# Turning the new keys and values into rows: matmuls with the identity, or square blocks on VectorE with stores that put them in place

## The chip, the cores and the metric

The kernel runs on one core of a Trainium2 chip. The metric is the time of one execution on the device, in microseconds, given as the median of three runs. The profile and the trace come from one further execution, taken by the hardware profiler. The engines are named as in the profile: PE is TensorE, DVE is VectorE, ACT is ScalarE, POOL is GpSimd, and SP is SyncE, which issues most of the DMAs.

## The reference

The reference computes one layer of a streaming encoder for 512 prompt frames and 64 sample frames of width 2048, all in 32-bit floats. Cut to what matters here, it is:

```python
proj = rmsnorm(x, g_norm1) @ w_in
q, k, v, gb, gc, hc = split(proj)              # q, k, v: 8 heads x 128; the rest: 8 groups x 128
q, k = rmsnorm(q, g_q), rmsnorm(k, g_k)        # per head
o_attn = stick_breaking(q, [k_past, k], [v_past, v])
o_conv = gb * conv3_causal(gc * hc)
x = x + concat(rmsnorm(o_attn), rmsnorm(o_conv)) @ w_out
x = x + (silu(h2 @ w_gate) * (h2 @ w_up)) @ w_down     # h2 = rmsnorm(x, g_norm2)
return x, k, v, new_conv
```

The new keys and values `k` and `v` are outputs of their own, as `k_prompt`, `v_prompt` (512 frames) and `k_sample`, `v_sample` (64 frames), each with one row of 128 numbers for a frame and a head. The change is about how these rows are made.

## The kernel before, in words

All activations are kept transposed: features lie on the 128 partitions, and the 576 frames (512 of the prompt, 64 of the sample) along the free axis. A product is a chain of matmuls with a tile of weights as the stationary operand and 288 frames as the moving one. For accuracy each operand is split into a high and a low part, so that each product of a weight tile with frames takes three matmuls; the high part is cast by ACT (L227) and the low one is a subtraction on DVE (L228). The large products use a Strassen-like scheme with seven partial products for each block of weights, and `prepare` (L357) makes the split weights of a product four products ahead of its use.

The work goes in stages. First the input is turned and the values of heads 0 to 3 are computed. Then, up to about 575 us, follow the 22 units listed in `HEADS_A` (L53): pairs of column blocks of `w_in`, for query and key of a head ("qk"), two value heads ("v"), or the convolution ("gh", "gb"). Then the output projection is computed with the attention woven into it, head by head, and at last the feed-forward network.

A finished key or value head is a tile `E` of 128 features by 576 frames. Its rows for the outputs are made by `tokens` (L804), a generator that is started with a lag when a head is done. It turns four blocks of 128 frames with matmuls against the identity into a bank of PSUM (L808), has ACT copy them to an SBUF tile `tok` (L810), and stores that with one DMA (L812). Three ticks later it turns the last 128 frames (L817), which ACT copies to `tokz` (L819), and stores the 64 sample rows (L820). For values it also stores both into `v_dram` (L814, L822), a buffer in device memory, from which the attention reads them again (`fetch_v`, L1031, called for head 0 at L1038 and for each later head at the end of the one before). `v_dram` holds, for each head, 128 partitions of five blocks of 128. `tokens` runs for the eight key heads and for value heads 4 to 7. Value heads 0 to 3 go through `plain_tokens` (L785), which scales the rows by the norm while ACT copies them; it too writes `v_dram`.

The tiles `tok` and `tokz` come from a pool with the tag "hl" and three buffers, which also serves squares, norms and the convolution (`hl_tile`, L628). A buffer is free again when its last reader, for a stored tile the DMA, is done.

PE's instructions run in the order in which the program writes them. The order of the others (ACT, DVE, POOL, SP) is set by the planner of the framework in the stages concerned here, from priorities and from its own view of what is ready. Each engine then works in its order and waits on semaphores. A small `Pipeline` (L73) counts ticks, one for every three matmuls of a product, and starts side work at given ticks.

At the seam to the attention stage the program calls `load_qk(0)` (L1035), `split_qk` (L1036), `load_cached_keys(0)` and `fetch_v(0)`. Their DMAs are issued by SP, as are the stores of `tokens` and the loads of `w_out` (L183). The first scores of a head are the matmuls at L1161.

Of the kernel before, what the change touches and what calls it, by code (L numbers as in the profile page):

```python
# [10 lines left out]
F32 = mybir.dt.float32  # L11
# [5 lines left out]
P = 128  # L17
TP = 512
TS = 64
T = TP + TS  # L20
HALF = T // 2
HALVES = ((0, HALF), (HALF, T))
D = 2048
KD = D // P
NH = 8
# [10 lines left out]
NFP = NFF // 2  # L36
DC = D // 256
SLOTS = 7
# [63 lines left out]
def tile_hybrid_stream_step(  # L102
# [6 lines left out]
    nc = tc.nc  # L109
# [22 lines left out]
    x2_dram = tc.dram_tile([KD, P, T], F32, name="x2_dram")  # L132
    hid_dram = tc.dram_tile([NFP, 2 * FORMS, P, HALF], F32, name="hid_dram")
    qk_dram = tc.dram_tile([NH, 2, P, T], F32, name="qk_dram")
    v_dram = tc.dram_tile([NH, P, 5, P], F32, name="v_dram")
    mixc_dram = tc.dram_tile([NG, P, 2, T], F32, name="mixc_dram")
    ps_pj = ctx.enter_context(tc.tile_pool(name="ps_pj", bufs=3, space=PSUM))
    ps_z = tc.alloc_tile_pool(name="ps_z", bufs=1, space=PSUM)
# [1 line left out]
    def misc(name):  # L140
        return ps_z.tile([P, 512], F32, tag="misc", name=name, bufs=2)
# [3 lines left out]
    for half in (1, 0):  # L145
        for c in range(D // 256):
            specs.append((w_out[half * AW : (half + 1) * AW, c * 256 : (c + 1) * 256]
# [46 lines left out]
    def next_weight():  # L194
        i = pos[0]
        pos[0] += 1
        end = first_block
        def pieces_of(j):
            hi, lo = weight_split(j)
            for a in range(0, 2048, 512):  # L200
                weight_parts(raws[j][:, :2048], hi, lo, a, a + 512, nc.vector)
                yield 7

        while len(raws) < min(i + 2, end):
            load_weight()
        if len(ready) <= i:
            split_weight(nc.vector)
        while len(raws) < min(i + 3, end):
            load_weight()
        if i + 1 < end:  # L210
            pipe.spawn(pieces_of(i + 1))
            pipe.run_due()
        out = ready[i]
        ready[i] = None
        return out
# [20 lines left out]
    ident = const.tile([P, P], F32, name="ident")  # L236
# [4 lines left out]
    rows = {}  # L241
# [307 lines left out]
    def turn_x(kt, low=None):  # L549
# [25 lines left out]
        if q == 0:  # L575
            for (a, b), d in zip(HALVES, (b11[:, j], b12a[:, j] if j < NP - 1 else b12b)):
                nc.scalar.activation(out=d[:, 0, :], in_=st[:, 0, a:b], func=AF.Copy, scale=g)
# [50 lines left out]
    def hl_tile(name):  # L628
        return tmp.tile([P, 2, HALF], F32, tag="hl", name=name, bufs=3).rearrange("p i t -> p (i t)")

    LAG = 3
    with tc.manual_schedule(engines={mybir.EngineType.Activation, mybir.EngineType.DVE, mybir.EngineType.SP}):
# [60 lines left out]
        for kt in range(KD + LAG):  # L693
# [22 lines left out]
            if kt in (7, 11, 17):  # L716
                j = (kt - 7) // 4
# [7 lines left out]
        for c in range(2):  # L725
            for i, (a, b) in enumerate(HALVES):
                if i:
# [12 lines left out]
        for kt in range(KD):  # L740
# [6 lines left out]
            if kt == 9:  # L747
                nc.vector.reduce_sum(out=ssr, in_=ssx, axis=mybir.AxisListType.X)
                nc.vector.tensor_scalar(out=ssr, in0=ssr, scalar1=1.0 / D, scalar2=EPS, op0=ALU.mult, op1=ALU.add)
                nc.gpsimd.tensor_tensor(out=rst, in0=ssr, in1=nhalf, op=ALU.pow)  # L750
# [15 lines left out]
    for c in range(2):  # L766
        for i, (a, b) in enumerate(HALVES):
            nc.scalar.copy(out=e1[c][:, a:b], in_=v1ps[c][i])
# [16 lines left out]
    def plain_tokens(E, h, lag):  # L785
        yield lag
        pa = misc("tok_p")
        for i in range(4):
            nc.tensor.transpose(pa[:, i * P : (i + 1) * P], E[:, i * P : (i + 1) * P], ident)
        t = hl_tile("tokp")[:, :TP].rearrange("p (i d) -> p i d", d=P)  # L790
        for i in range(4):
            nc.scalar.activation(out=t[:, i, :], in_=pa[:, i * P : (i + 1) * P], func=AF.Copy, scale=rst[:, i : i + 1])
        nc.sync.dma_start(out=vp[:, h, :].rearrange("(i p) d -> p i d", p=P), in_=t)
        nc.sync.dma_start(out=v_dram[h][:, :4, :], in_=t)
        nc.sync.dma_start(out=v_dram[h][: P - TS, 4, :], in_=t[TS:, 3, :])
        yield 3
        pb = misc("tok_q")
        nc.tensor.transpose(pb[:TS, :P], E[:, TP:T], ident)
        tz = hl_tile("toks")[:TS, :P]
        nc.scalar.activation(out=tz, in_=pb[:TS, :P], func=AF.Copy, scale=rst[:TS, 4:5])  # L800
        nc.sync.dma_start(out=vs[:, h, :], in_=tz)
        nc.sync.dma_start(out=v_dram[h][P - TS :, 4, :], in_=tz)

    def tokens(E, dst, dst_s, dram, lag):  # L804
        yield lag
        pa = misc("tok_a")
        for i in range(4):
            nc.tensor.transpose(pa[:, i * P : (i + 1) * P], E[:, i * P : (i + 1) * P], ident)  # L808
        ta = hl_tile("tok")[:, :TP]
        nc.scalar.copy(out=ta, in_=pa)  # L810
        ta = ta.rearrange("p (i d) -> p i d", d=P)
        nc.sync.dma_start(out=dst.rearrange("(i p) d -> p i d", p=P), in_=ta)  # L812
        if dram is not None:
            nc.sync.dma_start(out=dram[:, :4, :], in_=ta)  # L814
        yield 3
        pb = misc("tok_b")
        nc.tensor.transpose(pb[:, :P], E[:, T - P : T], ident)  # L817
        tb = hl_tile("tokz")[:, :P]
        nc.scalar.copy(out=tb, in_=pb[:, :P])  # L819
        nc.sync.dma_start(out=dst_s, in_=tb[TS:, :])  # L820
        if dram is not None:
            nc.sync.dma_start(out=dram[:, 4, :], in_=tb)  # L822

    ctile, utile, etile, seen = {}, {}, {}, {}
    accc = []
# [24 lines left out]
    def group_scale(acc_, bufs):  # L850
        for a, b in HALVES:
            ss = misc("ssg")[:, :HALF]
            mm(ss, oner.bitcast(F32), acc_[:, a:b], start=True, stop=True)
            yt = tmp.tile([P, 2, HALF], F32, tag="hl", name="ytg", bufs=bufs)
            y, t = yt[:, 0], yt[:, 1]
            nc.scalar.activation(out=ss, in_=ss, func=AF.Identity, scale=1.0 / (8 * P), bias=epsc)
            nc.scalar.activation(out=y, in_=ss, func=AF.Ln)
            nc.scalar.activation(out=y, in_=y, func=AF.Exp, scale=-0.5)
            nc.scalar.activation(out=t, in_=y, func=AF.Square)
            nc.vector.scalar_tensor_tensor(out=t, in0=t, scalar=-0.5, in1=ss, op0=ALU.mult, op1=ALU.mult)  # L860
            nc.vector.scalar_tensor_tensor(out=acc_[:, a:b], in0=t, scalar=1.5, in1=y, op0=ALU.add, op1=ALU.mult)
            yield 1
# [11 lines left out]
    def a_done(n, c, i, ps, part):  # L874
        kind, g = UNITS[n][:2]
        a, b = HALVES[i]
        if kind in ("v", "qk"):
# [83 lines left out]
    for E, h, lag in ((e1[0], 2, 8), (e1[1], 3, 22), (e0[0], 0, 36), (e0[1], 1, 50)):  # L961
        pipe.spawn(plain_tokens(E, h, lag))
# [50 lines left out]
    vtok = bpool.tile([P, 5, P], F32, name="vtok")  # L1013
# [15 lines left out]
        nc.sync.dma_start(out=cK, in_=ck[:, h, :].rearrange("(i p) d -> p i d", p=P))  # L1029

    def fetch_v(h):  # L1031
        nc.sync.dma_start(out=vtok, in_=v_dram[h])
        nc.sync.dma_start(out=cV, in_=cv[:, h, :].rearrange("(i p) d -> p i d", p=P))

    load_qk(0)  # L1035
# [31 lines left out]
    for h in range(NH):  # L1067
        t = tpool.tile([P, 2, T], F32R, tag=f"t{h}", name=f"mixa{h}")
# [5 lines left out]
    def out_proj(frame, R, after=None, before=None, first=None):  # L1074
        for c in range(D // 256):
            whi, wlo = first[0] if first and c == 0 else next_weight()
            load_x2()
            if before:
                before(c)
            for j in range(2):  # L1080
                kt = 2 * c + j
                for a, b in HALVES:
                    if first and kt == a == 0:
                        ps = first[1]
                    else:
                        ps = ps_pj.tile([P, HALF], F32, tag="pj", name="pjo")
                        product(ps, whi, wlo, slice(j * P, (j + 1) * P), frame, 8, a, b)
                    if first and c < PLAIN:
                        nc.vector.tensor_tensor(out=x2(kt)[:, a:b], in0=ps, in1=R[:, a:b], op=ALU.mult)
                        continue  # L1090


                    def finish_out(wait, ps=ps, kt=kt, a=a, b=b):
                        yield wait
                        nc.vector.tensor_tensor(out=ps, in0=ps, in1=R[:, a:b], op=ALU.mult)
                        nc.vector.tensor_tensor(out=x2(kt)[:, a:b], in0=ps, in1=x2(kt)[:, a:b], op=ALU.add)

                    pipe.spawn(finish_out(3 if after and kt == a == 0 else 0))
                    pipe.run_due()
                if first and j and c < PLAIN:  # L1100
                    nc.gpsimd.dma_start(out=x2t[c], in_=xt_dram[2 * c : 2 * c + 2].rearrange("k p t -> p k t"),
                                        accum_op=ALU.add)
                if after:
                    after(kt)
# [280 lines left out]
    def before_b2(c):  # L1385
        if c == 3:
            load_columns([("B", 0), ("B", 1)])
        elif c == D // 256 - 2:
            load_columns([("A", 0)])
# [305 lines left out]
```

## Time and profile before

| | us |
|---|---|
| three runs | 2346.91, 2347.15, 2348.15 |
| median | 2347.15 |
| the profiled execution, its own time | 2347.48 |
| the span of its profile | 2345.8 |

The time of an execution contains the span from its first instruction to its last, and a little around it. In the profile a line such as `L808 PE MATMUL tok_a<-ident,E` names the source line, the engine, the operation, and the tile written and those read. Rows of a timeline give the start, the duration, the engine and line, the operation, and in brackets how long the engine had been idle and what released it. `SPq` marks a DMA that is issued by SP: its duration is that of the issue, not of the transfer. The granted clock of PE was 1.000 throughout.

DMA engines moved 368.85 MB, 157 GB/s on average, of which 80.49 MB were written to device memory.

### The profile page before, as it was taken

What the parts mean: (1) busy time and instruction counts of PE and PEld (TensorE: products, weight loads), DVE (VectorE), ACT (ScalarE), POOL (GpSimd) and SP (SyncE); (2) the same over time, 40 slices, a digit from 0 to 9 for tenths busy, and PEclk for the clock granted to TensorE, in tenths of its full rate; (3) what the DMA queues carried; (4) which work ended last, traced back from release to release, by engine and by line L of the source; (5) the groups of instructions that cost most, each with busy time, mean ns of one, the idle gap of its engine ahead of it and who ended that gap; (6) DMA issues with size and microseconds to landing.
All of it is one profiled execution on the core that took longest, in us unless ns stands there. A gap on an engine that the chain in (4) does not pass through costs nothing. (4 is left out here: it accounts for less than half of the span.)

```text
span 2345.8 us, 43802 instructions
## 1 busy us (share of the span) xinstructions
PE 2332.0 (99%) x17561; PEld 2321.6 (99%) x17561; DVE 1940.0 (83%) x2834; ACT 1239.2 (53%) x2244; POOL 294.2 (13%) x374
## 2 busy tenths in 40 slices
PE   9999999999999999999999999999999999999999
PEld 8999999999999999999999999999999999999998
DVE  8889889797777898888888888888888778887875
ACT  8556656455887564444444444444444444444454
POOL 0211121120332320000000000000000002431211
PEclk9999999999999999999999999999999999999999
DMA  8444243436753454444444444444444937875642
GB/s 270 137 122 123 90 142 103 149 116 208 202 143 109 168 198 126 154 141 136 154 128 149 148 134 149 138 139 153 127 150 140 356 112 229 231 218 187 201 130 82
DMA packets 482867, 368.85 MB, mean 157 GB/s; under 512 B 11630, under 2 KB 465064, under 8 KB 482664
## 3 DMA queue, kind: packets, MB, share of 16 engines
q1 hardware_dynamic: 475848, 356.58, 47.5%
q0 software_dynamic: 6384, 9.21, 2.3%
q8 instruction: 137, 2.24, 0.4%
q14 instruction: 66, 0.54, 0.1%
q10 hardware_dynamic: 432, 0.27, 0.0%
HBM read 285.52 MB, written 80.49 MB: 156 GB/s over the span
## 5 line engine op out<-in xcount | busy, mean ns | idle before, releaser
L228 DVE TENSOR_TENSOR whl<-raw_a,whl 128x1024 fp32r<-128x1024 f32 (+4 forms) x384 | 435.8, 1135 | 61.2 <-ACT whl L227 59.9
L404 PE MATMUL psy<-t,whl 128*128 128x288 f32 x3000 | 449.8, 295 | 0.0
L227 ACT CAST whl<-raw_a 128x1024 fp32r<-128x1024 f32 (+4 forms) x384 | 360.0, 939 | 137.7 <-PE psx L404 46.4
L404 PE MATMUL psy<-h_s,whl 128*128 128x288 f32 x2766 | 417.4, 295 | 0.6 <-ACT part L427 0.6
L404 PEld LDWEIGHTS psy<-t,whl 128*128 128x128 f32 x3000 | 414.8, 188 | 0.2
L404 PE MATMUL psw<-t,whl 128*128 128x288 f32 x2688 | 390.3, 295 | 0.0
L404 PEld LDWEIGHTS psy<-h_s,whl 128*128 128x128 f32 x2766 | 383.7, 188 | 1.2 <-ACT part L427 1.1
L404 PEld LDWEIGHTS psw<-t,whl 128*128 128x128 f32 x2688 | 367.0, 188 | 0.2
L228 DVE TENSOR_TENSOR whl<-raw_b,whl 128x1024 fp32r<-128x1024 f32 (+5 forms) x234 | 253.3, 1083 | 88.0 <-ACT whl L227 87.1
L227 ACT CAST whl<-raw_b 128x1024 fp32r<-128x1024 f32 (+5 forms) x234 | 211.0, 904 | 211.0 <-issue 75.2
L427 ACT COPY part<-psy 128x288 f32<-128x288 f32 x309 | 122.8, 397 | 345.0 <-PE psy L404 343.8
L404 PE MATMUL psx<-h_s,whl 128*128 128x288 f32 x1164 | 170.9, 295 | 0.0
L227 ACT CAST whl<-s 128x1024 fp32r<-128x1024 f32 (+5 forms) x103 | 95.2, 925 | 122.8 <-PE psw L404 115.0
L404 PEld LDWEIGHTS psx<-h_s,whl 128*128 128x128 f32 x1164 | 159.8, 188 | 0.0
L404 PE MATMUL psy<-t12a,whl 128*128 128x288 f32 x1056 | 150.9, 296 | 0.0
L404 PE MATMUL psw<-t34a,whl 128*128 128x288 f32 x1056 | 150.6, 295 | 0.0
L404 PEld LDWEIGHTS psy<-t12a,whl 128*128 128x128 f32 x1056 | 143.5, 188 | 0.3
L404 PEld LDWEIGHTS psw<-t34a,whl 128*128 128x128 f32 x1056 | 143.7, 188 | 0.0
L228 DVE TENSOR_TENSOR whl<-s,whl 128x1024 fp32r<-128x1024 f32 (+5 forms) x103 | 109.8, 1066 | 20.2 <-ACT whl L227 19.5
L1439 POOL DMA_DIRECT2D hid_dram<-form x7 | 5.2, 738 | 954.1 <-DVE form L228 945.8
L223 PE MATMUL pjo<-mixc,whi 128*128 128x288 f32 x512 | 119.0, 300 | 0.0
L223 PE MATMUL pjo<-mixa,whi 128*128 128x288 f32 x512 | 102.8, 296 | 0.0
(591 smaller groups left out, 3953.3 us busy)
## 6 DMA issues: line engine op xcount, KB each, us to landing
hid_dram<-form SPq DMA_DIRECT2D x147, 288.0 KB, 2.8
raw_a<-in_w_in_dram SPq DMA_DIRECT2D x22, 1024.0 KB, 5.5
raw_b<-in_w_in_dram SPq DMA_DIRECT2D x22, 1024.0 KB, 6.1
raw_b<-in_w_gate_dram SPq DMA_DIRECT2D x22, 1024.0 KB, 7.8
raw_b<-in_w_up_dram SPq DMA_DIRECT2D x22, 1024.0 KB, 6.5
raw_a<-in_w_gate_dram SPq DMA_DIRECT2D x22, 1024.0 KB, 5.8
raw_a<-in_w_up_dram SPq DMA_DIRECT2D x22, 1024.0 KB, 5.5
h_s<-hid_dram SPq DMA_DIRECT2D x10, 2016.0 KB, 11.0
```

What stands on the lines that cost most here:

```text
L223: mm(ps, w_[:, k, csl], x_[:, a:b], start=(k == 0 and n == 0), stop=(k == nk - 1 and n == 2))
L227: cast = nc.scalar.copy(out=hi, in_=src)
L228: (lo_eng or nc.vector).tensor_tensor(out=lo, in0=src, in1=hi.bitcast(F32), op=ALU.subtract)
L404: mm(ps, whl[:, w_, j, :], x_, start=(start and j == 0 and q == 0), stop=(j == len(xs_) - 1 and q == 2), skip_group_check=True)
L427: nc.scalar.copy(out=t, in_=st["y"])
L1439: q.dma_start(out=hid_dram[fp][2 * n - 2 : 2 * n].rearrange("f p t -> p f t"), in_=t.bitcast(F32))
```

## The change

`tokens` no longer uses PE and ACT. One DVE instruction, `nc.vector.transpose`, turns the whole tile `E` of 128 x 576 in square blocks of 32 x 32: after it, partition `g + j` of block column `t` holds frame `32 t + j` for the features `g` to `g + 31`. For each of the four groups of 32 partitions, DMAs then store the blocks to their places, in pieces of 32 numbers: the prompt rows, the sample rows, and for values all 576 rows in `v_dram`. The second step, three ticks later, is gone.

`v_dram` now holds plain rows, 576 of 128 numbers for each head. `plain_tokens`, which still turns with PE, stores to it with two DMAs instead of three, and `fetch_v` reads it with two DMAs instead of one.

```diff
+BK = 32
...
-    v_dram = tc.dram_tile([NH, P, 5, P], F32, name="v_dram")
+    v_dram = tc.dram_tile([NH, T, P], F32, name="v_dram")
...
-        nc.sync.dma_start(out=v_dram[h][:, :4, :], in_=t)
-        nc.sync.dma_start(out=v_dram[h][: P - TS, 4, :], in_=t[TS:, 3, :])
+        nc.sync.dma_start(out=v_dram[h][:TP].rearrange("(i p) d -> p i d", p=P), in_=t)
...
-        nc.sync.dma_start(out=v_dram[h][P - TS :, 4, :], in_=tz)
+        nc.sync.dma_start(out=v_dram[h][TP:], in_=tz)
...
     def tokens(E, dst, dst_s, dram, lag):
         yield lag
-        pa = misc("tok_a")
-        for i in range(4):
-            nc.tensor.transpose(pa[:, i * P : (i + 1) * P], E[:, i * P : (i + 1) * P], ident)
-        ta = hl_tile("tok")[:, :TP]
-        nc.scalar.copy(out=ta, in_=pa)
-        ta = ta.rearrange("p (i d) -> p i d", d=P)
-        nc.sync.dma_start(out=dst.rearrange("(i p) d -> p i d", p=P), in_=ta)
-        if dram is not None:
-            nc.sync.dma_start(out=dram[:, :4, :], in_=ta)
-        yield 3
-        pb = misc("tok_b")
-        nc.tensor.transpose(pb[:, :P], E[:, T - P : T], ident)
-        tb = hl_tile("tokz")[:, :P]
-        nc.scalar.copy(out=tb, in_=pb[:, :P])
-        nc.sync.dma_start(out=dst_s, in_=tb[TS:, :])
-        if dram is not None:
-            nc.sync.dma_start(out=dram[:, 4, :], in_=tb)
+        t = hl_tile("tok")
+        nc.vector.transpose(out=t, in_=E)
+        for g in range(0, P, BK):
+            rows = t[g : g + BK].rearrange("j (t c) -> j t c", c=BK)
+            for a, b, to in ((0, TP, dst), (TP, T, dst_s), (0, T, dram)):
+                if to is not None:
+                    nc.sync.dma_start(out=to[:, g : g + BK].rearrange("(t j) c -> j t c", j=BK),
+                                      in_=rows[:, a // BK : b // BK])
...
     def fetch_v(h):
-        nc.sync.dma_start(out=vtok, in_=v_dram[h])
+        nc.sync.dma_start(out=vtok[:, :4], in_=v_dram[h][:TP].rearrange("(i p) d -> p i d", p=P))
+        nc.sync.dma_start(out=vtok[:, 4], in_=v_dram[h][T - P :])
         nc.sync.dma_start(out=cV, in_=cv[:, h, :].rearrange("(i p) d -> p i d", p=P))
```

## The prediction

> **What bounds the kernel now.** I read the page first: the busy shares, then the chain that ended last.
>
> ```profile
> span 2345.8 us, 43802 instructions
> ...
> PE 2332.0 (99%) x17561; PEld 2321.6 (99%) x17561; DVE 1940.0 (83%) x2834; ACT 1239.2 (53%) x2244; POOL 294.2 (13%) x374
> ...
> PE 20%; DVE 0%; issue 0%; POOL 0%; POOLq 0%; ACT 0%; ACTq 0%; DVEq 0%
> ```
>
> TensorE (PE) works 2332.0 of 2345.8 us, and the chain, which is followed back over the last fifth of the span, is PE alone. The view of the waits, asked for PE alone, shows what is left to lose or win:
>
> ```profile
> PE psx L555 <- DMA xin<-in_x_prompt_dram: 4.0, 1, 4.0
> PE psv L404 <- ACT part L427: 1.3, 1, 1.3
> PE zs L1205 <- DVE spl L228: 1.0, 3, 0.4
> ```
>
> In total they are 4.0, 1.3 and 1.0 us; all others are smaller. So PE is never short of work after its start, its order is fixed by hand, and two rules follow: every PE instruction taken out shortens the run by its own time, and every microsecond that PE is made to wait is added in full. Work on the other engines counts only where it arrives too late for PE.
>
> **What the change takes out.** `tokens` runs 12 times (8 key heads, value heads 4 to 7; heads 0 to 3 go through `plain_tokens` and keep their matmuls with the identity). Each run loses five such matmuls. The timeline of PE around the fourth:
>
> ```profile
> 297.78 0.56 PE L404 MATMUL psy<-bod,whl 128*128 128x288 f32 x3
> 298.17 0.60 PE L808 MATMUL tok_a<-ident,E-14_3268 128*128 128x128 f32 x4
> ...
> 299.83 0.27 PE L817 MATMUL tok_b<-ident,E-14_3268 128*128 128x128 f32 x1
> ...
> 301.56 3.33 PE L404 MATMUL psw<-t34a,whl 128*128 128x288 f32 x24
> 304.74 3.33 PE L404 MATMUL psx<-bod,whl 128*128 128x288 f32 x24
> ```
>
> The second column overlaps (matmuls are pipelined), so I go by starts. A product of 24 matmuls takes 304.74 - 301.56 = 3.18 us alone and 301.56 - 297.78 = 3.78 us with the five turns inside it: 0.60 us for one run of `tokens`, **12 x 0.60 = 7.2 us** off PE. That is the whole gain to be had.
>
> ScalarE (ACT) loses the two copies of each run, and SyncE (SP, which issues the DMAs) its two stores, four for a value head:
>
> ```profile
> L810 ACT COPY tok<-tok_a x12: 575/582/591, 161.5 to 583.2; 128x512 f32<-128x512 f32 x12
> L812 SPq DMA_DIRECT2D out_dram<-tok x12: 383/388/1362, 162.3 to 584.2; - x12
> ...
> L819 ACT COPY tokz<-tok_b x12: 246/266/273, 161.9 to 586.8; 128x128 f32<-128x128 f32 x12
> L820 SPq DMA_DIRECT2D out_dram<-tokz x12: 472/510/979, 163.7 to 587.1; - x12
> ```
>
> ACT gains 12 x (0.58 + 0.27) = 10.2 us; I count it as nothing, because PE waits for ACT only once for 1.3 us, ahead of all this.
>
> **What it adds on VectorE (DVE).** One turn of 128x576 for each run. The trace of before has none. The nearest row by size, and the load of the stage:
>
> ```profile
> 605.47 0.75 DVE L228 TENSOR_TENSOR spl<-hbl,sph 128x576 fp32r<-128x576 f32 x1
> 100.00:570.00 470.00, 470.00 (x3553) 469.74 (x3553) 409.55 (x542) 268.65 (x457) 75.27 (x81) 1.00 0.41 126
> 177.46 1.22 DVE L228 TENSOR_TENSOR whl<-raw_a,whl 128x1024 fp32r<-128x1024 f32 x1
> 182.40 0.82 PE L404 MATMUL psy<-bod,whl 128*128 128x288 f32 x5
> ```
>
> I take 0.75 us; the low end is nothing beyond what the engine idles, the high end 3.0 us, four passes of that row. DVE is busy 409.55 of 470 us in this stage, so 12 x 0.75 = 9 us fit into its 60 us of idle time. What hides them is the lead of the weight halves: the split that starts at 177.46 ends at 178.68, and the product that reads it starts at 182.40, a lead of 3.7 us, the smallest that I found from 100 us on. If a turn and the waits behind it together exceed that, PE waits.
>
> The Trainium skill's "VectorE: DVE Perf Modes", section "The three transpose paths", gives 311 ns for a 128x128 turn of bf16 on VectorE and says it goes in 32x32 blocks only. Scaled to 4.5 squares that is an estimate of 1.4 us; the sum below would be 0.65 us higher by it. No row of before can decide.
>
> **What it adds on the DMA side.** Each store now takes 32 rows of the turned tile and writes pieces of 32 numbers, 128 bytes. A key head issues 8 stores for 2, a value head 12 for 4: 8 x 6 + 4 x 8 = 80 issues more. The turned tile stays in one of three "hl" buffers until the last has landed. Before, such waits show already:
>
> ```profile
> 167.16 0.52 DVE L945 TENSOR_TENSOR oc<-psy,c 128x224 f32<-128x224 f32 x2 [1.66 <-DMA mixc_dram<-mc]
> 168.03 0.46 DVE L942 TENSOR_TENSOR oc<-psw,part 128x288 f32<-128x288 f32 x1 [0.35 <-DMA out_dram<-tokz]
> ```
>
> One buffer less is taken (tok and tokz become one), so the first of these waits should go, and the second become a wait for the eight stores, some 3.5 us. DVE is then late by 3.5 + 0.75 - 2.0 = 2.2 us, inside the lead of 3.7. I cost stage A at nothing, with 1.5 us of cover left at its thinnest place.
>
> **The seam to the attention stage** is where cover is missing. SP works in order, and the loads of head 0 (qf, kf) stand behind the stores of value head 6 and key head 7:
>
> ```profile
> 564.44 0.32 SPq L846 DMA_DIRECT2D qk_dram<-E  x1
> 571.56 2.36 DVE L176 TENSOR_TENSOR wlo<-raw_a,whi 128x1024 fp32r<-128x1024 f32 x2
> 572.99 0.39 SPq L812 DMA_DIRECT2D out_dram<-tok  x1
> 573.43 0.50 SPq L814 DMA_DIRECT2D v_dram<-tok  x1
> 574.46 0.51 SPq L820 DMA_DIRECT2D out_dram<-tokz  x1
> 575.02 1.23 SPq L822 DMA_DIRECT2D v_dram<-tokz  x1
> 576.34 0.39 SPq L183 DMA_DIRECT2D raw_a<-in_w_out_dram  x1
> 576.82 0.53 SPq L846 DMA_DIRECT2D qk_dram<-E-2_6479  x1
> 578.51 0.39 SPq L812 DMA_DIRECT2D out_dram<-tok  x1
> 579.45 0.51 SPq L820 DMA_DIRECT2D out_dram<-tokz  x1
> 580.01 0.68 SPq L1021 DMA_DIRECT2D qf<-qk_dram  x1
> 585.42 0.62 ACT L227 CAST qh<-qf 128x512 fp32r<-128x512 f32 x1 [1.66 <-DMA qf<-qk_dram]
> 586.07 0.69 DVE L228 TENSOR_TENSOR ql<-qf,qh 128x512 fp32r<-128x512 f32 x1 [1.62 <-ACT qh L227]
> 586.94 0.69 DVE L228 TENSOR_TENSOR kl<-kf,kh 128x512 fp32r<-128x512 f32 x1 [0.18 <-ACT kh L227]
> 587.69 0.39 PE L1161 MATMUL z<-qh,kl 128*128 128x256 f32 x1 [0.34 <-DVE kl L228]
> ```
>
> The issue of qf at 580.01 starts with SP unbroken from the store before it; qf lands, ACT waits 1.66 us for it, DVE follows, and PE already waits 0.34 us at the first scores. There is no slack on this path: what delays qf delays PE. In the clock of before: DVE is in the wlo splits until 573.84, so the turn of value head 6 ends about 574.6. A store costs SP 0.39 to 0.58 us and a gap of 0.05; I take 0.55. Twelve are 6.6 us (581.2), the weight load and the qk store 1.1 (582.3), eight for key head 7 4.4 (586.7). qf goes out 6.7 us later than 580.01, the scores start at 594.4 for 587.69. PE, rid of three turns since 571.6, would be there at 587.35 - 1.8 = 585.55, and waits 8.85 us, 0.34 of which it waited before. What is queued behind the qf load on SP (kf, the cached keys, the values, the stores of value head 7, the next weights) is late too; after the wait PE is late with it, so I add nothing more, 1 us at most. Were SP's planner to put qf ahead of the stores, this term would vanish.
>
> The reads of the values become two DMAs for each head, 8 issues more of about 0.5 us:
>
> ```profile
> SPq L1033 <- PE zs L1282: 32.1, 5, 9.7
> ```
>
> SP waits there for PE anyway, 32.1 us in five of eight heads, so they cost nothing.
>
> **Sum.** Own time of the profiled execution 2347.48 us (span 2345.8 and 1.7 around it; the median of the three runs is 2347.15). 2347.48 - 7.2 + 8.85 - 0.34 = **2348.8 us**. The price of an issue decides: at 0.45 us qf is 2 us earlier (2346.8), at 0.70 us 3 us later (2351.8). About 0.2%, 4.7 us, is what a measurement of this kernel can tell from no change, so this is "same".
>
> **Rivals.**
> 1. *The gain stays.* The planner orders ACT, DVE and SP by what it thinks ready, not by program order alone. If it puts qf and kf ahead of both heads' stores, PE loses nothing: 2347.48 - 7.2 = 2340.3. For it: in the rows SP has free time between 564.8 and 572.99. Against: before, it used none of it for qf. Ahead of key head 7 alone: 4.4 us less, 2344.4.
> 2. *Slower: the small pieces bind.* The mean price of a packet comes from this row:
>
> ```profile
> q1 hardware_dynamic: 475848, 356.58, 47.5%
> ```
>
> 0.475 x 16 x 2345.8 us / 475848 = 37.5 ns for 749 bytes on average. By bytes, 128 would cost 6.4 ns; by count, 37.5 ns. I take about 15 ns, since the row's large packets must carry most of its time, and then issuing is the limit. Value head 6 has 4608 pieces and key head 7 2304, 288 and 144 for each of 16 engines. At 37.5 ns these are 10.8 and 5.4 us in place of 6.6 and 4.4: 5.2 us more at the seam, **2354.0**, and 2 to 3 more where buffers come back late at the two heads after it. It decides from the price at which 432 pieces take 11.0 + 3.4 us: 33 ns. The Trainium skill's "DMA: Bandwidth & Descriptors", section "Specifications", speaks against this change: it wants at least 512 bytes for full rate, and below that it has the engine read, modify and write. No row of before has pieces of 128 bytes.
> 3. *Slower in stage A.* A turn of 2 to 3 us, or late buffers, use up the 3.7 us lead at up to 12 places; at 0.5 to 1 us each 2354 to 2361.
>
> **Chances.** Forecast (2346.8 to 2351.8, with a tail beyond 2352.2) 0.42; loads partly ahead, 2344, 0.10; full gain 0.16; small pieces 0.20; stage A 0.12. Faster by over 0.2% 0.19, within 0.44, slower 0.37: the forecast gives 0.05 of its 0.42 to slower, the partial case 0.03 to faster. The likeliest case by itself spans 2346 to 2352. The range takes in the full gain and the packet price at its upper end with its followers: 2340 to 2357.
>
> **What would show it.** No L808 or L817 group, PE busy about 7 us lower; a DVE group of 12 with 128x576; `qf` issued some 18 to 20 stores after the turn of head 6, and one PE wait of 8 to 9 us at L1161 on kl in the waits. If that wait is under 3 us, the seam was misread (rival 1). Landings of the 128-byte stores over 6 us, or stores issued more than 0.7 us apart, mean rival 2; waits at L404 on whl between 150 and 560 us mean rival 3. Wrong altogether would be a changed stage after 760 us.

## The result, and the profile after

| | before | after |
|---|---|---|
| median of 14 runs each, us | 2346.48 | 2352.02 |
| lowest and highest, us | 2345.59, 2348.62 | 2350.85, 2354.41 |
| the profiled execution, its own time, us | 2347.48 | 2351.58 |
| span, us | 2345.8 | 2349.9 |

The ratio is 1.0024 with an interval of 1.0017 to 1.0031: 5.5 us slower by the medians, 4.1 us by the two profiled executions. The forecast was 2348.8, with a range of 2340 to 2357: the time lies inside, on the slower side of the bound of 4.7 us and just above the likeliest case, which ended at 2351.8.

The page of the changed kernel, the lines that answer to those of before:

```profile
span 2349.9 us, 43762 instructions
...
PE 2327.9 (99%) x17501; PEld 2318.3 (99%) x17501; DVE 1946.1 (83%) x2846; ACT 1231.6 (52%) x2220; POOL 298.5 (13%) x374
...
q1 hardware_dynamic: 511496, 356.32, 48.1%
```

PE has 60 matmuls less, as meant, but its busy time falls by 4.1 us and not by 7. The second half of this section shows why: some of its matmuls ran at half clock and lasted longer. There are 35648 packets more on the queue, and the time of all of them rises by (0.481 x 2349.9 - 0.475 x 2345.8) x 16 = 256 us of DMA engine: 7.2 ns for each packet more, not 37.5. Not all of these are pieces of 128 bytes: 6720 of them come with the rows and the two reads alone (482568 packets in experiment e below).

The view of the waits of PE in the changed kernel (time in all, times, longest), and the same view for 100 to 560 us alone:

```profile
PE z L1153 <- ACT kh L228: 7.5, 1, 7.5
...
PE zs L1274 <- ACT ws L1202: 1.4, 1, 1.4
```

```profile
PE ss L284 <- DVE s L883: 0.7, 1, 0.7
```

The wait at the first scores is there, and it is the only long one behind the start. From 100 to 560 us PE waits once, for 0.7 us, and never for a weight half: the VectorE turns are paid for by the idle time there. A second wait, of 1.4 us for `ws`, is new and was not forecast.

The view of the tile `tok` in the changed kernel (for each group the shortest, the median and the longest in ns; the first of the 12 turns, which took 767 to 780 ns):

```profile
L812 SPq DMA_DIRECT2D out_dram<-tok x96: 315/487/2537, 160.8 to 591.9; - x96
...
L807 DVE STREAM_TRANSPOSE tok<-E-20_1697 x1: 778/778/778, 159.0 to 159.0; 128x576 f32<-128x576 f32 x1
...
DMA to landing us min/median/max: 1.5/2.1/6.2
```

A turn takes 0.77 us, where the subtraction of the same size gave 0.75. Stores land in 2.1 us in the median, sooner than the whole ones before (3.9 us for `tok`, 3.1 for `tokz`). But some issues take up to 2.5 us. At the seam the longest takes 1.7 us. The timeline of SP, ACT and PE there (a row with x2 or x8 has several issues):

```profile
567.98 0.38 SPq L184 DMA_DIRECT2D raw_a<-in_w_out_dram  x1
568.66 0.87 SPq L812 DMA_DIRECT2D out_dram<-tok  x2
...
570.09 2.46 SPq L812 DMA_DIRECT2D out_dram<-tok  x2
...
577.60 0.43 SPq L837 DMA_DIRECT2D qk_dram<-E-2_6452  x1
...
578.43 3.92 SPq L812 DMA_DIRECT2D out_dram<-tok  x8
582.40 0.43 SPq L1012 DMA_DIRECT2D qf<-qk_dram  x1
...
585.34 0.62 ACT L228 CAST qh<-qf 128x512 fp32r<-128x512 f32 x1 [6.99 <-DMA qf<-qk_dram]
...
586.79 0.58 PE L1153 MATMUL z<-qh,kh 128*128 128x256 f32 x1 [7.55 <-ACT kh L228]
```

SP works through the 12 stores of value head 6 from 568.66 until the store of a key at 577.60, then the 8 of key head 7 until 582.35, and only then issues the load of `qf`. ACT waits 6.99 us for it, and PE 7.55 us for ACT. This is the picture of the forecast.

What follows the wait isn't in the forecast. The view by windows (PE, PEld, DVE, ACT and POOL busy, then the granted clock, the DMA share and GB/s), at the seam and 70 us later:

```profile
580.00:585.00 5.00, 0.00 (x0) 0.00 (x0) 0.00 (x0) 0.00 (x0) 0.00 (x0) 0.77 0.56 131
585.00:590.00 5.00, 3.06 (x12) 2.77 (x13) 1.68 (x3) 2.41 (x5) 0.00 (x0) 0.50 0.94 246
590.00:595.00 5.00, 5.00 (x27) 4.86 (x27) 2.11 (x5) 2.90 (x9) 1.38 (x3) 0.71 0.46 79
595.00:600.00 5.00, 5.00 (x42) 5.00 (x42) 3.10 (x6) 4.36 (x10) 2.50 (x4) 1.00 0.70 217
...
660.00:665.00 5.00, 5.00 (x30) 5.00 (x29) 2.82 (x6) 4.09 (x10) 2.05 (x4) 0.66 0.53 143
```

PE's clock, at 1.00 until 580 us, falls to one half while PE idles, and PE resumes at half clock: from 590 to 595 it starts 27 matmuls, from 595 to 600 it starts 42. The same happens at 660 us, just behind the wait for `ws`. The timeline there:

```profile
648.67 0.38 SPq L184 DMA_DIRECT2D raw_a<-in_w_out_dram  x1
...
649.72 0.37 SPq L1023 DMA_DIRECT2D vtok<-v_dram  x1
...
658.44 0.30 ACT L228 CAST vz<-vtok 128x128 fp32r<-128x128 f32 x1 [3.62 <-DMA vtok<-v_dram]
658.64 0.43 ACT L1202 ACTIVATE ws<-zs 128x320 f32<-128x320 f32 x1
```

The read of the next head's values is now two DMAs. The first no longer waits for the last product of the head, so it goes out early, 1 us behind a load of 1 MB of weights, and ACT gets its data 8.7 us later. ACT's order has the cast of these values ahead of the exponential that makes `ws`, so PE waits for `ws`.

Where the time is lost can be read from the start of one instruction in both traces, here the first scores of heads 1 and 4, before and after (for head 0 it is 587.69 against 587.52, the product with `kl`):

```profile
605.78 0.27 PE L1161 MATMUL z<-qh,kl 128*128 128x256 f32 x1
668.16 0.28 PE L1161 MATMUL z<-qh,kl 128*128 128x256 f32 x1
```

```profile
608.07 0.28 PE L1153 MATMUL z<-qh,kl 128*128 128x256 f32 x1
675.38 0.28 PE L1153 MATMUL z<-qh,kl 128*128 128x256 f32 x1
```

The changed kernel is 0.17 us ahead at head 0, 2.29 behind at head 1, 7.22 behind at head 4, and 4.1 behind at the end: 3 us come back behind the fourth head, where the kernel before has waits of its own, the largest 1.3 us at 885 us. So some 2.5 us are lost right behind the seam wait, and about 2 more by the end. The windows from head 0's product to head 1's, first in the kernel before and then in the changed one, show what the 2.5 us are:

```profile
587.69:605.78 18.09, 18.09 (x135) 17.88 (x136) 12.95 (x27) 14.74 (x32) 6.81 (x12) 1.00 0.90 254
```

```profile
587.52:608.07 20.55, 20.55 (x136) 20.32 (x137) 11.90 (x25) 14.64 (x32) 6.66 (x12) 0.87 0.76 190
```

PE is busy all the time in both and waits for nothing. The clock is 0.87 on average in the changed kernel, which is 20.55 x 0.13 = 2.7 us lost: in this execution the 2.5 us are the half clock, not late loads.

### The profile page after: what moved, and what is told of

Its sections match the earlier page's. It is cut to its first block, busy times and chain, and to the rows that moved or that the text cites. A ratio compares the mean times of both kernels' runs of the same rounds, so it can differ in the third digit from the quotient of the medians.

```text
span 2349.9 us, 43762 instructions
## 1 busy us (share of the span) xinstructions
PE 2327.9 (99%) x17501; PEld 2318.3 (99%) x17501; DVE 1946.1 (83%) x2846; ACT 1231.6 (52%) x2220; POOL 298.5 (13%) x374
```

## The experiments

The theory: PE gains its turns in full; SP's extra issues at the seam take that back; and the two reads of the values cost a second, smaller wait. The rivals: the small pieces cost, wherever they are; the VectorE turns cost; the seam can't be faster for other reasons. The experiments ran on several chips. Ratios are against runs of the kernel before on the same chip, and experiments are best compared by them; its medians there were 2346.4 (beside c, d, a and f), 2346.8 (a2, b, e, g), 2346.05 (k, h, n) and 2346.3 (m).

| experiment | median, us | ratio, interval |
|---|---|---|
| c: kernel before, stores cut by partitions | 2352.67 | 1.0027 (1.0017 to 1.0037) |
| d: kernel before, stores cut by columns | 2356.70 | 1.0041 (1.0027 to 1.0054) |
| a: after, qf and kf of head 0 issued by POOL | 2349.59 | 1.0011 (1.0002 to 1.0019) |
| a2: after, all loads of head 0 issued by ACT | 2350.74 | 1.0018 (1.0009 to 1.0026) |
| f: after, PE's wait filled | 2353.88 | 1.0030 (1.0018 to 1.0041) |
| b: after, last three heads by PE | 2344.28 | 0.9989 (0.9980 to 0.9998) |
| e: kernel before, rows and two reads only | 2348.65 | 1.0008 (0.9999 to 1.0017) |
| g: after, cast of values behind ws | 2351.70 | 1.0021 (1.0012 to 1.0029) |
| k: after, reads in the other order | 2351.32 | 1.0022 (1.0013 to 1.0030) |
| h: b and k together | 2342.53 | 0.9985 (0.9976 to 0.9994) |
| n: stores of two heads issued by POOL | 2370.65 | 1.0104 (1.0090 to 1.0117) |
| m: h with each VectorE turn done twice | 2348.90 | 1.0008 (0.9999 to 1.0017) |

### c and d: the number of issues, and the size of the pieces

c, in `tokens` of the kernel before (the sample rows in four parts of 16 in the same way, `v_dram` in two):

```diff
-        nc.sync.dma_start(out=dst.rearrange("(i p) d -> p i d", p=P), in_=ta)
+        for g in range(0, P, 32):
+            nc.sync.dma_start(out=dst.rearrange("(i p) d -> p i d", p=P)[g : g + 32], in_=ta[g : g + 32])
```

> The kernel before, turns still by PE and ACT, with each store of tok and tokz cut by partitions into as many DMAs as the changed kernel issues (8 for a key head, 12 for a value head), with pieces of 512 bytes as before. Theory (the number of issues ahead of head 0's loads is what costs): 14 issues more at the seam at 0.55 us, 7.7 us of PE's wait, and half clock behind it, 3 us: 2346.5 + 10.7 = 2357. Rival (the pieces of 128 bytes cost, not the issues): no change, 2346 to 2347.

d, the same number of DMAs, cut by columns:

```diff
+        for g in range(0, P, 32):
+            nc.sync.dma_start(out=dst[:, g : g + 32].rearrange("(i p) c -> p i c", p=P), in_=ta[:, :, g : g + 32])
```

> The kernel before with the stores cut into as many DMAs as in the experiment with cuts by partitions, but by columns: the outputs are stored in pieces of 128 bytes, v_dram in pieces of 256. Theory (issues cost, pieces don't): the same time as with cuts by partitions within 1 us, about 2357. Rival (pieces cost): slower than the cut by partitions by 3 us or more, with landings over 6 us.

The timeline at the seam in c, with SP's four prompt stores of key head 7, the load of `qf` and PE's first scores; then the same in d:

```profile
581.55 2.22 SPq L813 DMA_DIRECT2D out_dram<-tok  x4
...
587.02 0.42 SPq L1025 DMA_DIRECT2D qf<-qk_dram  x1
...
591.25 0.58 PE L1165 MATMUL z<-qh,kh 128*128 128x256 f32 x1 [4.31 <-ACT kh L227]
```

```profile
582.67 3.63 SPq L813 DMA_DIRECT2D out_dram<-tok  x4
...
589.53 0.58 SPq L1025 DMA_DIRECT2D qf<-qk_dram  x1
...
594.04 0.58 PE L1165 MATMUL z<-qh,kh 128*128 128x256 f32 x1 [6.53 <-ACT kh L227]
```

In c nothing differs from the kernel before but 80 issues more: no small piece, no VectorE turn, no other layout. `qf` goes out at 587.02 and not at 580.01: 14 issues, 7.0 us, 0.50 us each. The kernel is 6.3 us slower. So issues alone do it, and the rival that only small pieces cost has fallen. The expected 2357 was too high by 4: the wait is 4.3 us and not 7.7. The loads land sooner: from the issue of `qf` to the first scores 4.2 us pass and not 7.0, and the DMA engines are 0.76 busy from 585 to 590 us, where the kernel before had 1.05 from 580 to 585. That the one makes the other isn't shown apart. Here too the half clock adds to the wait: PE is 4.3 us behind the kernel before at the first scores and 6.6 us behind after 3.5 us more of its work, without another wait.

d is 4.0 us slower than c, so my second statement, that pieces cost nothing, has fallen too. Four stores of key head 7 keep SP for 3.63 us and not 2.22. No store landed late: the cost is in the issue. The size of the pieces alone isn't it either, for in the changed kernel eight stores with pieces of 128 bytes, taken from 32 partitions each and not from 128, took 3.92 us, 0.49 each. What makes the issue longer in d stays open.

### a and a2: head 0's loads on another queue

```diff
-        nc.sync.dma_start(out=qf, in_=qk_dram[h, 0])
-        nc.sync.dma_start(out=kf, in_=qk_dram[h, 1])
+        eng = nc.gpsimd if h == 0 else nc.sync
+        eng.dma_start(out=qf, in_=qk_dram[h, 0])
+        eng.dma_start(out=kf, in_=qk_dram[h, 1])
```

> The changed kernel with head 0's two loads (qf, kf) issued by POOL instead of SP, so that they no longer stand behind the stores; nothing else differs. Theory (SP's queue at the seam): in the changed kernel PE idles 7.9 us before the first scores, and then runs at half clock for the 6 us that follow, some 3 us more. Both go, less about 1 us for POOL's slower issue: 2352.0 - 7.9 - 3 + 1 = 2342, and the granted clock at the seam is 1.0. Rival (small pieces, or VectorE's turns, cost over the whole stage): the wait at the scores moves elsewhere and the time stays at 2350 to 2352. Second rival (the reads of the values cost as much as the seam): 2346 to 2348.

a2 moves all six loads of head 0, to `nc.scalar`.

> The changed kernel with all six loads of head 0 (qf, kf, cK, the two of vtok, cV) issued by ACT, which idles at the seam, instead of SP; with qf and kf alone moved to POOL, PE's wait had moved to the cached keys (3.8 us for cK). Theory (everything of head 0 that stands behind the stores on SP is late, not only qf and kf): no wait over 1 us at the seam, the clock 1.0 until 655 us, and 2347.5 - 7.2 = 2340 plus 1.7 us for the late ws of head 2: 2341 to 2343. Rival (the seam can't be faster than in the kernel before, for other buffers become free no earlier): a wait of the same length on other tiles, 2347 to 2350.

The first line of PE's waits in a, and then in a2:

```profile
PE kc L1135 <- DMA cK<-in_cache_k_dram: 6.4, 2, 3.8
```

```profile
PE kc L1137 <- DMA cK<-in_cache_k_dram: 8.1, 1, 8.1
```

SP's timeline in a2, from the last store of value head 7:

```profile
592.10 1.37 SPq L812 DMA_DIRECT2D v_dram<-tok  x1
...
594.60 0.40 SPq L1023 DMA_DIRECT2D cK<-in_cache_k_dram  x1
```

By the medians both are faster than the changed kernel, by 2.4 and 1.3 us, though the intervals of the ratios overlap with its own, and both miss what I expected. In a the first scores start 7 us earlier, and PE then waits for the cached keys of heads 0 and 1, whose loads were left on SP. In a2 the waits of head 0 are gone, and one of 8.1 us stands at the cached keys of head 1, which SP loads at 594.60, behind the 12 stores of value head 7. So it is not six loads that are late but SP: it has more to issue from 568 to 595 us than it has time for, and whatever comes next on it is late. This sharpens the theory: once the first wait is taken away, the next load on SP is the one that PE waits for.

### f: is the half clock a cost of its own?

```diff
+        if h == 0:
+            fill = misc("fill")[:, :HALF]
+            for n in range(46):
+                mm(fill, mixc[:, n % 8, 0, :P], mixc[:, n % 8, 1, :HALF], start=True, stop=True)
```

> The changed kernel with 46 products of 128x288 into an unused bank (about 6.1 us of PE at full clock) put on PE ahead of head 0's first scores, where it waits for 7.9 us. Their result is not used. Theory (the half clock behind the wait comes from PE's idle time): the wait shrinks to about 1.5 us, the scores start when they did, the clock stays at 1.0 at the seam, and the time falls by what the half clock cost, 3 us, to 2349. Rival (the half clock comes from something else at this place, such as the load of the other engines or the transfers): half clock as before, and 2352 or, with the filling at half clock, up to 2358.

The scores and the next wait in f's timeline, and two of its windows:

```profile
587.91 0.38 PE L1153 MATMUL z<-qh,kh 128*128 128x256 f32 x1 [1.27 <-ACT kh L228]
...
595.91 1.10 PE L1185 MATMUL zs<-qf,kcT 128*128 128x64 f32 x8 [1.92 <-ACT kcT L1135]
```

```profile
590.00:595.00 5.00, 3.99 (x29) 3.72 (x27) 1.98 (x5) 2.87 (x8) 1.39 (x3) 1.00 0.59 101
595.00:600.00 5.00, 4.09 (x22) 4.09 (x23) 2.21 (x5) 3.91 (x9) 1.29 (x3) 0.70 0.54 134
```

The filling kept the clock at 1.00 through the wait, as the theory of the idle time wants. It gained nothing. At full clock PE runs into the next late thing, the turned cached keys (1.92 us), and then the clock falls all the same, from 597 to 600. From the first scores of head 0 to those of head 2 PE takes 42.2 us in f and 42.2 us in the changed kernel, against 38.5 in the kernel before. So the half clock follows idling, but it isn't 3 us that one could simply have back: in the changed kernel it stands in the place of waits that come without it. That f is 1.9 us slower by the medians isn't due to this place: in its trace `qf` goes out at 583.65 and not at 582.40, so it was 1.2 us late ahead of the seam.

### b: no extra issues at the seam

The part left out has the five matmuls with the identity, the two copies and the two or four whole stores of the kernel before, into plain rows.

```diff
+        turned.append(1)
+        late = len(turned) > 9
+        if late:
...
+            return
```

> The changed kernel with the last three heads (value head 6, key head 7, value head 7) turned by PE and stored whole, as before; the other nine by VectorE; v_dram in plain rows. Theory (the issues at the seam are the whole cost, the turns taken off PE a real gain): PE loses 9 turns, 5.4 us, the seam is as in the kernel before, and the late ws of head 2 costs 1.7 us: 2346.5 - 5.4 + 1.7 = 2342.8. Rival (the stage up to 560 us pays with the stores in small pieces, or the gain is lost at the seam in another way): 2346 or more.

The load of `qf` in b's timeline:

```profile
575.70 0.59 SPq L1035 DMA_DIRECT2D qf<-qk_dram  x1
```

With the last three heads turned by PE again, it goes out 6.7 us earlier than in the changed kernel, there is no wait at the first scores, and the kernel is faster than the kernel before: 0.9989 (0.9980 to 0.9998). So the turns taken off PE are a real gain where SP has room. It is 1.5 us short of the expected 2342.8. In its profiled execution PE waits 2.2 us for `ws`, with half clock behind it; but this execution, 2346.68, was the slowest of its eleven, so it doesn't show what the median lost.

### e, g and k: the reads of the values

e is the kernel before with the rows and the two reads alone (the diff of `v_dram`, `plain_tokens` and `fetch_v` above, and `tokens` storing to plain rows).

> The kernel before with one part of the change alone: v_dram in plain rows, and each head's values read back with two DMAs instead of one; all turns stay on PE and ACT. Theory (the first of the two loads is issued before the scores' sample part, lands late, and ACT is planned to cast it ahead of ws): PE waits some 1.4 us for ws at one head near 650 us, with a dip of the clock behind it, and 2346.5 + 1.5 to 3 = 2348 to 2349.5. Rival (this wait comes from the delay at the seam, not from the reads): no such wait, 2346 to 2347.

g, in the changed kernel (`behind` is the exponential that makes `ws`, and what is written under it stays behind it in ACT's order):

```diff
-            split_v()
+            with tc.issue_after(behind):
+                split_v()
```

> The changed kernel with the cast of the next head's values on ACT put behind the exponential that makes ws; nothing else differs. Theory (ACT's order there costs the 1.4 us of wait at 659 us and the half clock behind it): the wait and the dip of the clock at 660 us go, 2352.0 - 1.4 - 1.7 = 2349. Rival (PE is late there for another reason, or gives it back later): 2351 to 2353.

k, in the changed kernel:

```diff
-        nc.sync.dma_start(out=vtok[:, :4], in_=v_dram[h][:TP].rearrange("(i p) d -> p i d", p=P))
-        nc.sync.dma_start(out=vtok[:, 4], in_=v_dram[h][T - P :])
+        last = nc.sync.dma_start(out=vtok[:, 4], in_=v_dram[h][T - P :])
+        with tc.issue_after(last.ins):
+            nc.sync.dma_start(out=vtok[:, :4], in_=v_dram[h][:TP].rearrange("(i p) d -> p i d", p=P))
```

> The changed kernel with the two reads of a head's values issued in the other order: the last block first, which waits for the samples' products, and the four others behind it, so that both go out when the one read of the kernel before did. Theory (the early read lands late behind a load of weights, and the order planned for it costs 1.4 us of wait and a dip of the clock near 660 us): the wait for ws and the dip go, nothing else changes: 2352.0 - 1.9, the price of the reads measured alone, = 2350. Rival (as when only the cast was moved: the wait shows up elsewhere): 2351.7 to 2352.5.

A line of PE's waits in e; then, for k, the line of the view of `vtok` that says how long engines waited for it (in the changed kernel it was 9.4 us, 5 times):

```profile
PE zs L1282 <- ACT ws L1210: 1.4, 1, 1.4
```

```profile
  DMA vtok<-v_dram: 1.6, 1
```

In e the wait for `ws` appears without any of the stores in pieces, so it comes from the rows and the reads. Its time, +1.9 us by the medians, is as expected, though the interval just includes no change. In g the wait for `ws` is gone and the time is not: the values still land late (up to 8.7 us), ACT waits 6.8 us for them, and PE has small waits at other places (0.8 us for `x`, 0.7 for `spl`). In k both reads go out late again, ACT hardly waits for them, and neither the wait for `ws` nor the half clock at 660 us is there. Yet k is only 0.3 us nearer to the kernel before than the changed kernel was (+5.3 against +5.5), with intervals that overlap; its profiled execution was 1.2 us shorter. So beside the delay at the seam the price of the reads can't be measured. The next experiment takes that delay away too:

### h: both costs taken away

> The last three heads turned by PE, the other nine by VectorE, and the reads of the values in the other order as in the experiment beside it. Theory (two costs, issues at the seam and the early read; both gone): 2346.5 - 9 x 0.60 = 2341, no wait of PE over 1 us after its start, clock 1.0 throughout. Rival (the late wait is not due to the reads): 2344, as with the last three heads by PE alone.

The longest of PE's waits in h from 560 to 765 us (four, together 1.3):

```profile
PE zs L1221 <- DVE spl L229: 1.3, 4, 0.4
```

h beats both kernels: 2342.53 us, 0.9985 (0.9976 to 0.9994) of the kernel before, and 9.5 us less than the changed kernel by the medians. Against the kernel before on its own chip it is 3.5 us faster, b 2.5: the order of the reads would be worth 1 us, but the intervals of b and h overlap, so this price isn't shown. No wait over 0.4 us is left in the attention stage. Nine turns at 0.60 us would be 5.4; the medians show 3.5, the two profiled spans 2345.8 - 2339.7 = 6.1 us, of which about 1 is a shorter start; the profiled execution of h was its fastest.

### n: the same stores from POOL

Value head 6 and key head 7 as in the changed kernel, but with `nc.gpsimd.dma_start` for their 20 stores; value head 7 by PE; the reads as in k.

> Value head 6 and key head 7 turned by VectorE as in the changed kernel, but their 20 stores issued by POOL, which idles for 20 us there, instead of SP; value head 7 by PE; the reads in the other order. The pieces and the number of DMAs ahead of the scores are those of the changed kernel. Theory (what costs at the seam is SP's time to issue): PE loses 11 turns, 2346.5 - 6.6 = 2340, no wait at the first scores. Rival (the transfers themselves, or the number of DMAs in flight, delay the loads whatever queue issues them): a wait of 4 us or more at the first scores and 2346 or more. A third way: POOL, at 0.56 to 0.75 us an issue, is late with its masks, 2343 to 2346.

POOL's first store, SP's load of `qf`, POOL's last store of value head 6 and PE's wait, in n's timeline:

```profile
571.45 1.42 POOL L836 DMA_DIRECT2D out_dram<-tok  x2 [38.47 <-DVE tok L831]
573.78 0.47 SPq L1036 DMA_DIRECT2D qf<-qk_dram  x1
...
604.48 0.68 POOL L836 DMA_DIRECT2D v_dram<-tok  x1 [1.28 <-issue]
...
619.52 0.79 PE L1240 MATMUL z<-pr,trir 128*128 128x128 f32 x2 [26.27 <-POOL pr L1191]
```

Two things at once. SP, rid of the stores, issues `qf` at 573.78, and the first scores no longer wait. This doesn't test the transfers as I had meant it to: POOL had issued 2 of the 20 stores by then, and not all 20. What speaks against the transfers is the changed kernel itself, where `qf` goes out behind all 20 stores and ACT has it 2.9 us later, sooner than in the kernel before (5.4 us). And POOL needs much longer than the 0.56 to 0.75 us of the loads that it issued in a: from 571.45 to 605.16 for the 12 stores of value head 6, 2.8 us each, and its masks, which stand behind all 20, make PE wait 26 us. The issues themselves take 0.55 to 0.86 us in the profile; the rest is 1.3 to 5.8 us between them, for which it shows no wait. The 8 stores of key head 7 take 1.1 us each, though half of them have 512 pieces too, so what makes POOL slow stays open. This is the third way that I had written down, at many times its size.

### m: twice the turns

```diff
         nc.vector.transpose(out=t, in_=E)
+        nc.vector.transpose(out=t, in_=E)
```

> The kernel with the last three heads by PE and the reads in the other order, with each of its nine VectorE turns done twice into the same tile. Theory (VectorE's turns are hidden behind the lead of the weight halves): 9 x 0.77 = 6.9 us more of VectorE, and the same time within 1 us, 2342.5. Rival (the turns are late for PE up to 560 us, at least in part, and eat up some of the gain): 2345 to 2349.5, with waits of PE on whl.

ACT at the same work in h's timeline, then in m's near 472 us, and PE's waits in m there:

```profile
465.75 2.02 ACT L228 CAST whl<-raw_a 128x1024 fp32r<-128x1024 f32 x2
```

```profile
472.04 0.47 ACT L851 ACTIVATE ss<-ss,epsc 128x288 f32<-128x288 f32 x1 [3.99 <-PE ss L284]
...
473.96 1.03 ACT L228 CAST whl<-raw_a 128x1024 fp32r<-128x1024 f32 x1
```

```profile
PE psy L405 <- ACT whl L228: 1.8, 1, 1.8
...
PE psy L405 <- DVE whl L229: 1.1, 1, 1.1
```

6.4 us slower than h, where I expected no change. It isn't VectorE's time: from 100 to 560 us PE has long waits at one place alone, near 472 us, and no turn runs within 25 us of it. There the order planned for ACT has become another: in h ACT makes three casts of weight halves ahead of this norm, in m one; then it idles 3.99 us for `ss` of the norm and does the norm's steps ahead of the casts of two weight halves, for which PE waits 2.9 us, with half clock behind it. The waits and the clock are 4.6 of the 7.5 us between the two profiled executions; 1.3 more are there before the first turn. The cover of this stage is real for work of 0.8 us, but the order of the other engines is planned anew with each change, and a bad place in it costs as much as the whole gain.

## Why the prediction was right or wrong

**PE's turns, 7.2 us: right.** Sixty matmuls are gone, and from turn to turn PE's lead on the kernel before grows by about 0.6 us, to 7.4 us at the seam. 1.1 us of this lead are a shorter start of the profiled execution, and 0.5 were lost to the one wait, so the turns gave 6.8. So the scores of head 0 start 0.17 us earlier than before although PE waited 7.55 us. b and h turn the gain into time. "PE waits for ACT only once" was read too narrowly (its waits before also show `part` twice more, 0.6 us), and nothing hung on it.

**VectorE's turn, 0.75 us: right.** It took 0.77 us. The estimate of 1.4 us, scaled from the 311 ns of the Trainium skill's "VectorE: DVE Perf Modes", section "The three transpose paths", is disproved for this shape: 0.77 us is the measurement, and the row by size was the better guide.

**Stage A at nothing: right** for this kernel (one wait of 0.7 us). The 3.5 us that VectorE was to wait for the eight stores did not come: up to 560 us no engine waits for a store of `tok`. m shows that the stage isn't safe.

**The seam: right in its mechanism, and nearly in size.** Forecast 8.85 us of wait, measured 7.55. `qf` went out 20 stores after the turn, as said. The eight stores took 0.49 us each; the 12 took 0.74, since some were stretched to 1.2 and 1.7 us. That is over the 0.7 us named as a sign of the small pieces, but c has the same stretch there with whole pieces (2.99 us for four stores). By the forecast `qf` would go out at 586.7 - 9 x 0.6 = 581.3; it was 582.40. What made up for it is the landing: before, 5.4 us passed from the issue of `qf` to ACT's cast, now 2.9. The windows of the kernel before fit this:

```profile
580.00:585.00 5.00, 5.00 (x41) 5.00 (x40) 3.32 (x6) 2.67 (x5) 0.00 (x0) 1.00 1.05 356
```

The DMA engines were busy throughout there (1.05), and about half as much in the changed kernel (0.56).

**"After the wait PE is late with it, so I add nothing more, 1 us at most": this is the step that failed.** The shift goes from -0.17 us at head 0 to +2.29 at head 1. Two things were left out, and in the measured execution the first alone cost time there. The first is the clock: PE has no wait in this stretch, but runs its first 5.4 us at half clock. The second is that what stands behind `qf` on SP is late by more than PE is, since value head 7's 12 stores come behind it too: a, a2 and f show PE waiting for something later each time that the first wait is taken away or filled. On the clock, the Trainium skill's "TensorE: Matmul & The Clock Gate", section "Part 1: The HAM clock gate (the "warmup" mystery)", says that PE falls to half clock after an idle window of about 3.4 us and comes back after a busy one. This trace agrees: PE idles from 579.25, the clock falls at 582.7, it is 0.77 on average from 580 to 585 and 0.50 from 585 to 590, and it is 1.00 again from 593. A forecast that has PE idle for 8.85 us should have had this rule as a term: by the skill's window at least 3.4 us at half clock, an estimate of 1.7 us lost. So a microsecond of wait was not just added in full, as the prediction's second rule has it: in c 4.3 us of wait cost 6.6.

**The two reads of the values, "they cost nothing": wrong.** I weighed the issue that was added and not that a read in two parts may start earlier, behind other traffic, and change ACT's order. It cost a wait of 1.4 us and a dip of the clock, 3.1 us where it stands (the shift is 3.9 us ahead of it and 7.0 behind), of which the later heads give back most. Alone it is about 1.9 us by the medians (e, with an interval that just includes none), and 1 us between b and h, whose intervals overlap: the wait is shown, its price in the whole time is not.

**The rivals.** The first, a full gain, needed SP to have room; h shows that it was to be had by leaving the seam alone. The second, small pieces at 37.5 ns, has fallen as stated: 7.2 ns for each packet more, and landings of 2.1 us in the median, with one of 6.2. But d shows that an issue can take longer with them. The third fell with the missing waits on `whl`.

So the direction came out right, and the size was short by 2.8 us on the profiled pair (+4.1 against +1.3): 1.5 us less up to the first scores, some 2.5 more right behind them, and about 2 more by the end, with the reads in it. Of the 1.5 us, 1.1 are the shorter start; without it the pair would be 5.2 us apart, near the 5.5 of the medians, against 1.3 forecast. That the time lies in the range owes much to the range, which was wide enough to take in the full gain and the rival of the small pieces: the two terms that were left out, some 2.5 and 2 us, are each larger than the forecast change.

## What to carry to other kernels

A matmul taken off a full TensorE is worth its whole time, but the DMAs that replace it cost about half a microsecond each on the queue that issues them: look for the place where that queue has something urgent next, and leave the change out there. Where a forecast contains a wait of PE, ask what else stands on the queue that caused it, and add the clock. Splitting a transfer also changes when its first part may start, and so the order of everything that waits for it.

## What was not expected of the hardware

- Half clock follows waits far shorter than the one at the seam. In the changed kernel a wait of 1.40 us at 659 us was followed by a clock of 0.66 from 660 to 665, in f one of 1.92 us by 0.70 from 595 to 600. In e and in a the same wait of 1.4 us had none behind it. Ahead of the end of PE's work, each stretch at half clock in these traces lasted 3.4 us or a multiple of it: 3.4 us at 661 us and 10.2 at the seam in the changed kernel, 6.8 in k, 3.4 twice in f. The section of the Trainium skill's "TensorE: Matmul & The Clock Gate" named above speaks of a free-running window, which would let the same wait hit or miss; that this decided here isn't shown.
- POOL issued the loads of two whole tiles in 0.56 and 0.75 us, but 12 stores in pieces of 128 bytes took it 2.8 us each, and the next eight 1.1.
- SP's issues, mostly 0.43 to 0.5 us each, stretch now and then, up to 2.5 us. The longest store (2.54 us, at 250.5 us) started 3.1 us behind a load of 1 MB, but one of 2.0 us (at 438.6 us) 8.9 us behind one. What stretches them stays open.
